# Token sums formed in place from PSUM, a fixed engine order behind the output product, each row normed with its residual

## The chip, the core and the metric

The kernel runs on one core of one Trainium2 chip. The metric is device time in microseconds (us), lower is better. A core has TensorE (PE, with its weight loads PEld), VectorE (DVE), ScalarE (ACT), GpSimd (POOL) and the queues that issue transfers (here mostly SP's). Each engine works through its own queue in order; they wait for each other on semaphores.

## What is computed

Two decoder layers on 1024 tokens of width 1024, float32. Each layer is a mixer, its output product, and a gated MLP, with an RMS norm before and after each half:

```python
for layer in range(2):
    y = mixer(rmsnorm(h, g[0]))                  # two mixers side by side, then one output product
    h = h + rmsnorm(y, g[1])
    y = conv_glu_ffn(rmsnorm(h, g[2]), w_up, conv_w, conv_b, w_down)
    h = h + rmsnorm(y, g[3])

def conv_glu_ffn(h, w_up, conv_w, conv_b, w_down):   # D_FF = 2816
    up = causal_depthwise_conv(h @ w_up, conv_w, conv_b)
    val, gate = split(up, 2)
    return (gelu(gate) * val) @ w_down
```

The change touches the stretch from the output product (`mix_out`) to the first chunk of the up product (`ffn`), and one place where the up product meets the down product (`down`). Both layers run the same code there.

## The kernel before

**Numbers in two parts.** Every operand of a large product is split into a high part (ACT, a copy to fp32r) and a low part (DVE, source minus high part): `split`, L88 to L90. `mm3` (L276) makes a product from three matmuls: high by high, high by low, low by high.

**The output product, `mix_out`.** Eight rows (t = 0 to 7) of 128 tokens. A row is 36 matmuls of 512 columns into a PSUM tile `pd`; then `residual` (row's sum of squares on ACT, a chain of small DVE operations for the root, two 1024-wide DVE operations, L270 and L271) and `prenorm` (again squares, root and L148). The norm of row t-1 is traced behind the residual of row t. `to_blocks` transposes a normed row on PE into a PSUM tile `pt` and splits it into the operands of the up product. Six rows go through `to_blocks` in `mix_out`, the last two in `ffn`.

**The up product, `ffn`.** It is a seven-product scheme on halves: tokens t < 4 and t >= 4, and input features in two halves. So it needs seven operands of tokens, `A[1]` to `A[7]`, and seven of weights for each of the 22 chunks of features. `A[1]` and `A[2]` are the plain first tokens, `A[4]` a negated part of the late tokens; `A[6]`, `A[7]`, `A[5]` and `A[3]` are differences and sums of an early and a late row (`sums`, `split_s4`). For them `to_blocks` keeps a copy `xr` of every row in SBUF (L386). The weights of a chunk arrive as two tiles `wr` (`up_raw`); `up_plain` splits the first (`w1`, for products 1 and 2), `up_sums` makes the others: `wt` for product 5, `w2` for 6 and 3, `w4` for 7 and 4. `prod` is one of the seven, 12 matmuls. Products 1 and 2 of a chunk (`p1`, `p2`) run LEAD = 2 chunks ahead of its other five (`chunk`).

So `ffn` starts with p1, p2 of chunks 0, 1 and 2, the last two rows' `to_blocks`, all token sums and chunk 0's weights; then it goes through `chunk(0)` to `chunk(21)`, each with products 6, 7, 5, 3 and 4 of its own and p1, p2 of the chunk two ahead (chunk 0 has none of these). A chunk ends with two convolutions, a gelu and the gating product L516, which is stored to DRAM.

**The down product, `down`,** is a generator. It prepares (loads, subtracts, splits: `prep`, L569) a list of operand pairs `made`, at first during the last two chunks.

**Order and room.** The program is traced in the order of the source; then a scheduler orders each engine's queue by its own estimate of times, and assigns buffers. `in_order` (L152), used at the kernel's start, ties PE's, ACT's and DVE's instructions of a block to the order in which they are traced. SBUF tiles come from two pools: `t4`, 21 tiles of 128x1024, and `t8`, 14 tiles of twice that (all 14 are the operands `A` from the first chunk on). PSUM has four tiles of 128x1024 (`ps`), for `pd`, `pt`, the accumulators `ac` of three chunks and `bb`.

Of the kernel before, what the change touches and what calls it, by code (L numbers as in the profile page):

```python
# [19 lines left out]
P = 128  # L20
# [25 lines left out]
class Trunk:  # L46
# [273 lines left out]
    def mix_out(self, layer, nk, hsrc, hdst):  # L320


        gpost = self.bcast(self.a["norm_g"][layer, 1], "gpost")
        gpre = self.bcast(self.a["norm_g"][layer, 2], "gpre", True)
        us = [self.unit(look=nk - 1 - j) for j in range(nk)]
        pend = []
        self.new_blocks(layer)
        for t in range(NT):
            sl = slice(t * P, (t + 1) * P)
            pd = self.PS("pd")  # L330
            for k in range(nk):
                for c in range(2):
                    cs = slice(c * 512, c * 512 + 512)
                    self.mm3(pd[:, cs], self.mix[k][0][:, sl], self.mix[k][1][:, sl], us[k][0][:, cs], us[k][1][:, cs], k == 0, k == nk - 1)
            hn = self.residual(t, pd, hsrc, hdst, gpost)
            if t:
                pend.append((t - 1, self.prenorm(last[0], gpre, last[1])))
            last = hn
            if t == 5:
                self.up_raw(0)  # L340
            if t == 6:
                self.up_plain(0)
            if t == 7:
                self.up_raw(1)
            if len(pend) > 1:
                self.to_blocks(*pend.pop(0))
        pend.append((NT - 1, self.prenorm(last[0], gpre, last[1])))
        return pend


# [16 lines left out]
    def to_blocks(self, t, xn):  # L367
        nc = self.nc
        pt = self.PS("pt").rearrange("p (k t) -> p k t", k=KD)
        for k in range(KD):  # L370
            nc.tensor.transpose(pt[:, k], xn[:, k * P:(k + 1) * P], self.ident)
        sl = slice(t % 4 * P, t % 4 * P + P)
        if t < 4:
            if t % 2 == 0:
                xr = self.T2("xr", F32, [P, 2, KD, P])
                self.xr[t], self.xr[t + 1] = xr[:, 0], xr[:, 1]
            for p in (1, 2):
                hi, lo = self.operand(p)
                self.split(hi[:, :, sl], lo[:, :, sl], pt[:, 4 * p - 4:4 * p])
        else:  # L380
            self.xr[t] = self.T("xr").rearrange("p (k t) -> p k t", k=KD)

            hi, lo = self.operand(4)
            nc.scalar.activation(hi[:, :, sl], pt[:, 4:], AF.Copy, scale=-1.0)
            nc.vector.scalar_tensor_tensor(lo[:, :, sl], pt[:, 4:], -1.0, hi[:, :, sl].bitcast(F32), op0=ALU.mult, op1=ALU.subtract)
        nc.scalar.activation(self.xr[t], pt, AF.Copy)  # L386

    def sums(self, t):


        v = self.nc.vector.tensor_tensor
        x, y = self.xr.pop(t - 4), self.xr.pop(t)
        sl = slice(t % 4 * P, t % 4 * P + P)
        if t % 2 == 0:
            self.s4 = self.T("s4").rearrange("p (j k t) -> p j k t", j=2, k=4)
        s32, s1 = (self.T("s").rearrange("p (j k t) -> p j k t", j=2, k=4) for _ in range(2))
        s3, s2, s1, s4 = s32[:, 0], s32[:, 1], s1[:, 0], self.s4[:, t % 2]
        v(s3, x[:, :4], y[:, :4], op=ALU.subtract)
        v(s2, y[:, 4:], s3, op=ALU.subtract)
        v(s1, y[:, :4], y[:, 4:], op=ALU.add)  # L400
        v(s4, x[:, 4:], s2, op=ALU.subtract)
        for p, src in ((6, s2), (7, s3), (5, s1)):
            hi, lo = self.operand(p)
            self.split(hi[:, :, sl], lo[:, :, sl], src)
        self.raw_sums[t] = s4

    def split_s4(self):
        hi, lo = self.operand(3)
        for t in range(4, NT):
            sl = slice(t % 4 * P, t % 4 * P + P)  # L410
            self.split(hi[:, :, sl], lo[:, :, sl], self.raw_sums[t])

    def up_raw(self, n):

# [12 lines left out]
        u[1], u[2] = self.parts(u["raw"][0], "w1")  # L427

    def up_sums(self, n):
        v = self.nc.vector.tensor_tensor  # L430
        u = self.up[n]
        r1, r2 = u.pop("raw")
        half = slice(0, 512)
        v(r2[:, half], r2[:, half], r1[:, half], op=ALU.subtract)
        t1 = self.T("wt", F32R)
        u[5] = t1[:, half], t1[:, 512:]
        self.split(*u[5], r2[:, half])
        v(r2[:, half], r2[:, 512:], r2[:, half], op=ALU.subtract)
# [13 lines left out]
    def ffn(self, layer, pend, hsrc, hdst, last):  # L452
        nc, a = self.nc, self.a
        add = lambda o, x, y: nc.vector.tensor_tensor(o, x, y, op=ALU.add)  # L454
        cw = self.small([P, 2 * NF, 4], "cw", bufs=1)
        nc.sync.dma_start(cw, a["ffn_cw"][layer])
        gd = [self.dr.tile([P, 2, 1024], F32, name=f"gd{layer}{m}") for m in range(NF // 2)]
        down = self.down(layer, gd, hsrc, hdst, last)
        lo, hi = slice(0, 512), slice(512, 1024)
        bb = {}  # L460

        def prod(out, n, p, first):
            w, x = self.up[n][p], self.A[p]
            for k in range(4):
                ks = slice(k * P, (k + 1) * P)
                self.mm3(out, w[0][:, ks], w[1][:, ks], x[0][:, k], x[1][:, k], first and k == 0, k == 3, True)

        def p1(n):
            u = self.up[n]
            u["ac"], u["val"], u["gate"] = self.PS("ac"), self.T("val"), self.T("gate")  # L470
            prod(u["ac"][:, lo], n, 1, True)
            nc.scalar.activation(u["val"][:, lo], u["ac"][:, lo], AF.Copy)

        def p2(n):
            u = self.up[n]
            if n % 2 == 0:
                bb[n // 2] = self.PS("bb")
            b = bb[n // 2][:, hi if n % 2 else lo]
            prod(b, n, 2, True)
            add(u["val"][:, lo], b, u["val"][:, lo])  # L480

        def chunk(n):
            u = self.up[n]
            val, gate = u["val"], u["gate"]
            A, C = u["ac"][:, lo], u["ac"][:, hi]
            m = n + LEAD
            if n == NF - 2:
# [5 lines left out]
            nc.scalar.activation(gate[:, hi], A, AF.Copy)
            add(gate[:, hi], C, gate[:, hi])
            if n and m < NF:
                p1(m)
            elif n:
                next(down)
            prod(A, n, 3, False)
            nc.scalar.activation(gate[:, lo], A, AF.Copy)  # L500
            if n and m < NF:
                p2(m)
            elif n:
                next(down)
            prod(C, n, 4, False)
            add(val[:, hi], C, val[:, hi])
# [21 lines left out]
        self.to_blocks(*pend.pop(0))
        self.sums(5)
        self.up_raw(2)  # L530
        self.sums(6)
        self.up_plain(2)
        p1(2)
        p2(2)
        self.sums(7)
        self.up_sums(0)
        self.split_s4()
        self.up_raw(3)
        for n in range(NF):
# [1077 lines left out]
```

## Time and profile before

| | us |
|---|---|
| median of 3 runs | 2282.49 (2278.32 to 2285.65) |
| the profiled execution | 2282.59 |
| its span | 2280.8 |
| PE busy in the span | 2161.2 |
| DVE busy in the span | 1589.6 |
| ACT busy in the span | 1050.7 |

The span is the time from the first instruction to the last in the trace, so 1.8 us of the profiled execution lie around it. A busy PE is not a PE at its peak: the array's clock has two levels, and the profile gives the granted clock of a stretch as a share of the full one.

### The profile page before, as it was taken

How to read it: one execution, taken by the hardware profiler on the slowest of the kernel's cores; microseconds unless marked ns; L12 is line 12 of the kernel's file. 1: busy time of each engine (PE TensorE's matmuls, PEld its weight loads, DVE VectorE, ACT ScalarE, POOL GpSimd, SP SyncE). 2: the span in 40 equal slices, each digit the busy share in tenths (PEclk: the TensorE clock that was granted, in tenths of full speed). 3: DMA queues.
4: the chain of work that ended last, by engine and by line, in shares of the span. 5: the costliest groups of instructions: out<-in, count | busy, mean ns of one | idle time of the engine just before them, and what ended most of it. 6: DMA issues, size and time to landing. Idle time of an engine off the chain costs nothing.

```text
span 2280.8 us, 25452 instructions
## 1 busy us (share of the span) xinstructions
PE 2161.2 (95%) x10096; PEld 1743.8 (76%) x10096; DVE 1589.6 (70%) x2083; ACT 1050.7 (46%) x1445; POOL 125.1 (5%) x101
## 2 busy tenths in 40 slices
PE   7899969999999999999999999999699999999997
PEld 6677847888887788788888877677588888877885
DVE  8877676777777787961234375667677777778787
ACT  5647444444445444540223375445454444444443
POOL 0550000000000000100000000410000000000001
PEclk9999979999999999999999999899799999999999
DMA  4012322222222530331011100434122222243304
GB/s 159 12 34 95 121 92 74 83 83 83 79 77 112 205 137 21 123 127 32 34 38 56 51 29 19 126 109 151 42 83 83 83 77 75 80 158 137 148 10 147
DMA packets 53896, 198.82 MB, mean 87 GB/s; under 512 B 7045, under 2 KB 8133, under 8 KB 51218
## 3 DMA queue, kind: packets, MB, share of 16 engines
q1 hardware_dynamic: 52130, 193.49, 23.7%
q0 software_dynamic: 1504, 3.46, 0.6%
q8 instruction: 79, 1.29, 0.2%
q14 instruction: 39, 0.32, 0.0%
q10 hardware_dynamic: 144, 0.26, 0.0%
HBM read 154.60 MB, written 41.99 MB: 86 GB/s over the span
## 4 chain that ended last, share of the span: by engine, by line
PE 47%; DVE 6%; ACT 3%; issue 1%; DMA 0%; DVEq 0%; SPq 0%; ACTq 0%
PE ac L279 5%; PE ac L281 5%; PE ac L280 5%; PE pj L279 4%; PE pj L280 4%; PE pj L281 4%; PE pd L280 3%; PE pd L279 3%; PE pd L281 3%; PE bb L279 1%; PE bb L280 1%; PE bb L281 1%; PE po L1242 1%; PE hpo L1454 1%; PE pi L279 1%
## 5 line engine op out<-in xcount | busy, mean ns | idle before, releaser
L279 PE MATMUL pj<-yh,wh 128*128 128x512 f32 (+1 forms) x672 | 266.6, 397 | 6.6 <-ACT s5uf L84 4.5
L280 PE MATMUL pj<-yl,wh 128*128 128x512 f32 (+1 forms) x672 | 260.9, 388 | 1.0 <-DVE yl L90 1.0
L281 PE MATMUL pj<-yh,wl 128*128 128x512 f32 (+1 forms) x672 | 259.5, 386 | 0.0
L280 PE MATMUL pd<-dwl,dgh 128*128 128x512 f32 x528 | 207.0, 392 | 6.8 <-DVE dwl L90 6.8
L281 PE MATMUL pd<-dwh,dgl 128*128 128x512 f32 x528 | 206.8, 392 | 0.0
L279 PE MATMUL pd<-dwh,dgh 128*128 128x512 f32 x528 | 206.3, 391 | 0.0
L279 PE MATMUL ac<-ah,w2h 128*128 128x512 f32 x352 | 143.9, 409 | 13.9 <-ACT w2h L89 11.1
L279 PEld LDWEIGHTS pj<-yh,wh 128*128 128x128 f32 x672 | 129.3, 192 | 34.1 <-ACT s5uf L84 4.7
L279 PE MATMUL ac<-ah,w4h 128*128 128x512 f32 x352 | 144.0, 409 | 5.5 <-ACT val L490 5.5
L280 PEld LDWEIGHTS pj<-yl,wh 128*128 128x128 f32 x672 | 129.0, 192 | 26.3 <-issue 3.4
L281 PEld LDWEIGHTS pj<-yh,wl 128*128 128x128 f32 x672 | 128.9, 192 | 25.6 <-issue 1.3
L281 PE MATMUL ac<-ah,w2l 128*128 128x512 f32 x352 | 139.6, 397 | 1.1 <-DVE w2l L90 1.1
L280 PE MATMUL ac<-al,w4h 128*128 128x512 f32 x352 | 139.1, 395 | 0.0
L280 PE MATMUL ac<-al,w2h 128*128 128x512 f32 x352 | 139.0, 395 | 0.0
L281 PE MATMUL ac<-ah,w4l 128*128 128x512 f32 x352 | 138.5, 393 | 0.0
L280 PEld LDWEIGHTS pd<-dwl,dgh 128*128 128x128 f32 x528 | 100.0, 189 | 28.5 <-DVE dwl L90 7.7
L281 PEld LDWEIGHTS pd<-dwh,dgl 128*128 128x128 f32 x528 | 100.0, 189 | 21.0
L279 PEld LDWEIGHTS pd<-dwh,dgh 128*128 128x128 f32 x528 | 99.5, 189 | 21.2 <-ACT dwh L89 0.4
L447 ACT ACTIVATE tv<-val,cw 128x1024 f32<-128x1024 f32 x44 | 54.8, 1246 | 127.9 <-DVE val L454 127.9
L89 ACT ACTIVATE dwh<-dw 128x1024 fp32r<-128x1024 f32 x66 | 69.9, 1059 | 93.0 <-PE pd L280 86.7
L515 ACT ACTIVATE tg<-tg 128x1024 f32<-128x1024 f32 x44 | 46.7, 1062 | 135.4 <-DVE tg L449 135.3
L649 POOL TENSOR_TENSOR acc<-acc,gpost 128x1024 f32<-128x1024 f32 x8 | 18.9, 2393 | 1512.9 <-ACT junk L646 1512.9
(441 smaller groups left out, 5151.9 us busy)
## 6 DMA issues: line engine op xcount, KB each, us to landing
wr<-in_WU_dram SPq DMA_DIRECT2D x88, 512.0 KB, 4.2
raw<-in_W_dram SPq DMA_DIRECT2D x56, 512.0 KB, 3.7
gd<-tv SPq DMA_DIRECT2D x44, 512.0 KB, 2.6
dg<-gd SPq DMA_DIRECT2D x20, 1024.0 KB, 5.1
dw<-in_WD_dram SPq DMA_DIRECT2D x20, 1024.0 KB, 7.6
h<-h SPq DMA_DIRECT2D x28, 512.0 KB, 4.3
h<-hn SPq DMA_DIRECT2D x20, 512.0 KB, 2.9
h<-in_x_dram SPq DMA_DIRECT2D x16, 512.0 KB, 4.7
```

Source lines behind the costliest of these rows:

```text
L89: self.nc.scalar.activation(hi, src, AF.Copy)
L279: mm(out, lhsT=lh, rhs=rh, start=first, stop=False, skip_group_check=chain)
L280: mm(out, lhsT=lh, rhs=rl, start=False, stop=False, skip_group_check=chain)
L281: mm(out, lhsT=ll, rhs=rh, start=False, stop=last, skip_group_check=chain)
L447: nc.scalar.activation(t0, src, AF.Identity, scale=cw[:, c, 2:3], bias=cw[:, c, 3:4])
L515: nc.scalar.activation(tg, tg, AF.Gelu_apprx_tanh)
L649: nc.gpsimd.tensor_tensor(acc[t], acc[t], gpost, op=ALU.mult)
L1242: nc.tensor.matmul(po[cols, c, at], lhsT=V(ku)[:, c, cols], rhs=st[:, hp, j], start=j == 0, stop=j == 1)
L1454: nc.tensor.matmul(po[rs, t], lhsT=qi[:, n * 64:n * 64 + 64], rhs=st[(n - 1) // 8][:, (n - 1) % 8], start=False, stop=True)
```

## The change

1. `mix_out`: row t is normed right behind its own residual instead of behind the residual of row t+1. The rows still wait two deep for `to_blocks`.
2. `to_blocks` for t >= 4 makes no copy of the row. It takes three sums on DVE straight from the PSUM tile: two into one new SBUF tile, the third in place over the early row's copy. `split_sum` splits one kind of sum for a list of rows; the sum for `A[3]` is made there, in place.
3. `up_sums` is cut in two: up to `w2` (`up_sums1`), and `w4` (`up_sums2`).
4. The start of `ffn` is traced in another order, under `in_order`; chunk 2's weights are requested first.
5. `chunk(0)` runs its last products as 5, 4, 3 and copies product 7 out first.
6. In `down`, the pairs number 4 to 11 are prepared under `issue_after` the last gating product: their DVE instructions stand behind it in DVE's queue.

```diff
             hn = self.residual(t, pd, hsrc, hdst, gpost)
-            if t:
-                pend.append((t - 1, self.prenorm(last[0], gpre, last[1])))
-            last = hn
+            pend.append((t, self.prenorm(hn[0], gpre, hn[1])))
...
-            if len(pend) > 1:
+            if len(pend) > 2:
                 self.to_blocks(*pend.pop(0))
-        pend.append((NT - 1, self.prenorm(last[0], gpre, last[1])))
...
-        else:
-            self.xr[t] = self.T("xr").rearrange("p (k t) -> p k t", k=KD)
...
-        nc.scalar.activation(self.xr[t], pt, AF.Copy)
...
+            nc.scalar.activation(self.xr[t], pt, AF.Copy)
+            return
+        hi, lo = self.operand(4)
+        nc.scalar.activation(hi[:, :, sl], pt[:, 4:], AF.Copy, scale=-1.0)
+        nc.vector.scalar_tensor_tensor(lo[:, :, sl], pt[:, 4:], -1.0, hi[:, :, sl].bitcast(F32), op0=ALU.mult, op1=ALU.subtract)
+        v = nc.vector.tensor_tensor
+        x = self.xr[t - 4]
+        y = self.xr[t] = self.T("xs").rearrange("p (k t) -> p k t", k=KD)
+        v(y[:, :4], x[:, :4], pt[:, :4], op=ALU.subtract)
+        v(y[:, 4:], pt[:, 4:], y[:, :4], op=ALU.subtract)
+        v(x[:, :4], x[:, :4], y[:, 4:], op=ALU.add)
+    def split_sum(self, p, rows):
+        src = {6: lambda x, y: y[:, 4:], 7: lambda x, y: y[:, :4], 5: lambda x, y: x[:, :4], 3: lambda x, y: y[:, 4:]}[p]
+        if p == 3:
+            for t in rows:
+                y = self.xr[t][:, 4:]
+                self.nc.vector.tensor_tensor(y, self.xr[t - 4][:, 4:], y, op=ALU.subtract)
+        hi, lo = self.operand(p)
+        for t in rows:
             sl = slice(t % 4 * P, t % 4 * P + P)
-            self.split(hi[:, :, sl], lo[:, :, sl], self.raw_sums[t])
+            self.split(hi[:, :, sl], lo[:, :, sl], src(self.xr[t - 4], self.xr[t]))
...
             prod(C, n, 7, True)
+            if n == 0:
+                nc.scalar.activation(gate[:, hi], C, AF.Copy)
             prod(A, n, 5, False)
...
+            if n == 0:
+                add(gate[:, hi], A, gate[:, hi])
+                prod(C, n, 4, False)
+                add(val[:, hi], C, val[:, hi])
+                prod(A, n, 3, False)
+                nc.scalar.activation(gate[:, lo], A, AF.Copy)
...
-        p1(0)
-        p2(0)
-        self.to_blocks(*pend.pop(0))
-        self.up_plain(1)
-        self.sums(4)
-        p1(1)
-        p2(1)
-        self.to_blocks(*pend.pop(0))
-        self.sums(5)
         self.up_raw(2)
-        self.sums(6)
-        self.up_plain(2)
-        p1(2)
-        p2(2)
-        self.sums(7)
-        self.up_sums(0)
-        self.split_s4()
+        with self.in_order():
+            p1(0)
+            p2(0)
+            self.up_plain(1)
+            self.up_sums1(0)
+            self.to_blocks(*pend.pop(0))
+            self.split_sum(6, (4, 5, 6))
+            p1(1)
+            p2(1)
+            self.up_plain(2)
+            self.to_blocks(*pend.pop(0))
+            self.split_sum(6, (7,))
+            p1(2)
+            self.up_sums2(0)
+            p2(2)
+            self.split_sum(7, range(4, NT))
+            self.split_sum(5, range(4, NT))
+            self.split_sum(3, range(4, NT))
         self.up_raw(3)
...
-            made.append(prep(b, p, len(made) > len(steps) // 2))
+            wide = len(made) > len(steps) // 2
+            if 4 <= len(made) < 12:
+                with self.tc.issue_after(self.gated.ins if hasattr(self.gated, "ins") else self.gated):
+                    made.append(prep(b, p, wide))
+            else:
+                made.append(prep(b, p, wide))
```

## Rows read from the trace of the kernel before

**Rows 1.** The page, first part: busy us, share of the span, instructions.

```profile
PE 2161.2 (95%) x10096; PEld 1743.8 (76%) x10096; DVE 1589.6 (70%) x2083; ACT 1050.7 (46%) x1445; POOL 125.1 (5%) x101
```

**Rows 2.** Four stages of layer 0: stretch, length, busy (count) by engine, granted clock.

```profile
core 0: us, PE busy (x) PEld busy (x) DVE busy (x) ACT busy (x) POOL busy (x), PEclk, DMA share, GB/s
217.65:288.60 70.95, 70.95 (x338) 59.09 (x337) 45.67 (x102) 33.94 (x61) 0.00 (x0) 1.00 0.33 113
288.60:332.95 44.35, 24.43 (x91) 18.55 (x90) 34.02 (x62) 22.70 (x39) 0.00 (x0) 0.74 0.31 105
332.95:356.31 23.36, 20.70 (x67) 15.20 (x68) 11.49 (x13) 6.22 (x8) 0.00 (x0) 0.76 0.14 46
356.31:450.00 93.69, 93.68 (x408) 75.58 (x407) 71.46 (x74) 47.46 (x56) 0.00 (x0) 1.00 0.20 74
```

**Rows 3.** What PE waited for, whole span: total us, times, longest.

```profile
PE ac L279 <- ACT w1h L89: 24.9, 4, 9.0
...
PE pd L280 <- DVE dwl L90: 6.8, 2, 3.4
```

**Rows 4.** PE in order of time, layer 0: start, us, instruction, idle before.

```profile
288.61 0.48 PE L279 MATMUL ac<-ah,w1h 128*128 128x512 f32 x1
...
296.24 1.66 PE L371 MATMUL pt<-cst,h 128*128 128x128 f32 x8 [1.94 <-DVE h L148]
...
319.54 0.80 PE L279 MATMUL ac<-ah,w1h 128*128 128x512 f32 x1 [9.04 <-ACT w1h L89]
...
332.95 0.79 PE L279 MATMUL ac<-ah,w2h 128*128 128x512 f32 x1 [5.53 <-ACT w2h L89]
...
356.50 0.39 PE L281 MATMUL ac<-ah,w2l 128*128 128x512 f32 x1
```

**Rows 5.** Two stretches behind a wait, columns as in Rows 2.

```profile
301.30:306.80 5.50, 5.48 (x14) 4.33 (x15) 4.39 (x6) 0.63 (x1) 0.00 (x0) 0.50 0.89 278
...
332.90:344.00 11.10, 9.80 (x21) 6.82 (x22) 4.72 (x6) 1.66 (x2) 0.00 (x0) 0.50 0.00 0
```

**Rows 6.** ACT in order of time, layer 0.

```profile
300.22 1.05 ACT L89 ACTIVATE w1h<-wr 128x1024 fp32r<-128x1024 f32 x1
...
318.45 1.04 ACT L89 ACTIVATE w1h<-wr 128x1024 fp32r<-128x1024 f32 x1
```

**Rows 7.** DVE groups, 288.6 to 356.6: count, busy us, mean ns, idle before.

```profile
L398 DVE TENSOR_TENSOR s<-xr 128x512 f32<-128x512 f32 x4 | 2.7, 686 | 0.0
...
L148 DVE SCALAR_TENSOR_TENSOR h<-hn,rn,gpre 128x1024 f32<-128x1024 f32 x2 | 2.6, 1278 | 0.0
...
L385 DVE SCALAR_TENSOR_TENSOR al<-pt,ah 128x512 fp32r<-128x512 f32 x3 | 2.1, 686 | 1.0 <-ACT ah L384 1.0
```

**Rows 8.** DVE in order of time: two neighbours of each width.

```profile
302.44 0.68 DVE L398 TENSOR_TENSOR s<-xr 128x512 f32<-128x512 f32 x1
303.05 0.68 DVE L400 TENSOR_TENSOR s<-xr 128x512 f32<-128x512 f32 x1
...
333.46 1.22 DVE L90 TENSOR_TENSOR w2l<-wr,w2h 128x1024 fp32r<-128x1024 f32 x1
334.59 0.69 DVE L90 TENSOR_TENSOR al<-s,ah 128x512 fp32r<-128x512 f32 x1
```

**Rows 9.** SP's queue in order of time, layer 0.

```profile
286.74 1.26 SPq L417 DMA_DIRECT2D wr<-in_WU_dram  x2
...
300.48 0.33 SPq L124 DMA_DIRECT2D gpre<-in_norm_g_dram  x1
300.91 26.68 SPq L417 DMA_DIRECT2D wr<-in_WU_dram  x4
```

**Rows 10.** PE in layer 1: its first up-product matmul, and chunk 1's.

```profile
1584.86 0.48 PE L279 MATMUL ac<-ah,w1h 128*128 128x512 f32 x1
...
1650.47 0.39 PE L281 MATMUL ac<-ah,w2l 128*128 128x512 f32 x1
```

**Rows 11.** DVE where the up product meets the down product, layer 0.

```profile
763.33 1.23 DVE L573 TENSOR_TENSOR dw<-dw 128x1024 f32<-128x1024 f32 x1 [3.03 <-DMA dw<-in_WD_dram]
764.47 0.69 DVE L454 TENSOR_TENSOR val<-ac,val 128x512 f32<-128x512 f32 x1
```

More of the change, by code (lines that the diff above doesn't have):

```diff
@@ L379, in to_blocks @@
                 self.split(hi[:, :, sl], lo[:, :, sl], pt[:, 4 * p - 4:4 * p])
-        else:
-            self.xr[t] = self.T("xr").rearrange("p (k t) -> p k t", k=KD)
-            hi, lo = self.operand(4)
-            nc.scalar.activation(hi[:, :, sl], pt[:, 4:], AF.Copy, scale=-1.0)
-            nc.vector.scalar_tensor_tensor(lo[:, :, sl], pt[:, 4:], -1.0, hi[:, :, sl].bitcast(F32), op0=ALU.mult, op1=ALU.subtract)
-        nc.scalar.activation(self.xr[t], pt, AF.Copy)
[L388 to L405, printed above, removed]
@@ L407, in split_s4 @@
-    def split_s4(self):
-        hi, lo = self.operand(3)
-        for t in range(4, NT):
+            nc.scalar.activation(self.xr[t], pt, AF.Copy)
[6 more added lines that the diff above has]
+        y = self.xr[t] = self.T("xs").rearrange("p (k t) -> p k t", k=KD)
@@ L429, in up_sums, with up_sums1 @@
     def up_sums(self, n):
+        self.up_sums1(n)
+        self.up_sums2(n)
+    def up_sums1(self, n):
         v = self.nc.vector.tensor_tensor
         u = self.up[n]
-        r1, r2 = u.pop("raw")
+        r1, r2 = u["raw"]
         half = slice(0, 512)
@@ L438, in up_sums, with up_sums2 @@
         v(r2[:, half], r2[:, 512:], r2[:, half], op=ALU.subtract)
+        u[6], u[3] = self.parts(r2, "w2")
+    def up_sums2(self, n):
+        u = self.up[n]
+        r1, r2 = u.pop("raw")
         r1 = r1.rearrange("p (j c) -> p j c", j=2)
-        v(r1, r2[:, half].unsqueeze(1).to_broadcast([P, 2, 512]), r1, op=ALU.subtract)
-        u[6], u[3] = self.parts(r2, "w2")
+        self.nc.vector.tensor_tensor(r1, r2[:, :512].unsqueeze(1).to_broadcast([P, 2, 512]), r1, op=ALU.subtract)
         u[7], u[4] = self.parts(r1.rearrange("p j c -> p (j c)"), "w4")
@@ L491, in chunk @@
             prod(C, n, 7, True)
+            if n == 0:
+                nc.scalar.activation(gate[:, hi], C, AF.Copy)
             prod(A, n, 5, False)
[L493 to L506, printed above, removed]
+            if n == 0:
[5 more added lines that the diff above has]
+            else:
+                nc.scalar.activation(gate[:, hi], A, AF.Copy)
+                add(gate[:, hi], C, gate[:, hi])
+                p1(m) if m < NF else next(down)
+                prod(A, n, 3, False)
+                nc.scalar.activation(gate[:, lo], A, AF.Copy)
+                p2(m) if m < NF else next(down)
+                prod(C, n, 4, False)
+                add(val[:, hi], C, val[:, hi])
             if m + 1 < NF:
@@ L515, in chunk @@
             nc.scalar.activation(tg, tg, AF.Gelu_apprx_tanh)
-            nc.vector.tensor_tensor(tv, tv, tg, op=ALU.mult)
+            self.gated = nc.vector.tensor_tensor(tv, tv, tg, op=ALU.mult)
             nc.sync.dma_start(gd[n // 2][:, n % 2], tv)
             self.up.pop(n)
-        p1(0)
-        p2(0)
-        self.to_blocks(*pend.pop(0))
-        self.up_plain(1)
-        self.sums(4)
-        p1(1)
-        p2(1)
-        self.to_blocks(*pend.pop(0))
-        self.sums(5)
-        self.up_raw(2)
-        self.sums(6)
-        self.up_plain(2)
-        p1(2)
-        p2(2)
-        self.sums(7)
-        self.up_sums(0)
-        self.split_s4()
+        self.up_raw(2)
+        with self.in_order():
[16 more added lines that the diff above has]
+            self.split_sum(3, range(4, NT))
         self.up_raw(3)
@@ L618, in more @@
                 load(b, {2: 1, 1: 0}[p])
-            made.append(prep(b, p, len(made) > len(steps) // 2))
+            wide = len(made) > len(steps) // 2
+            if 4 <= len(made) < 12:
+                with self.tc.issue_after(self.gated.ins if hasattr(self.gated, "ins") else self.gated):
+                    made.append(prep(b, p, wide))
+            else:
+                made.append(prep(b, p, wide))
         def room(cap):
```

## The prediction

> **What bounds the kernel now.** The busy shares come first: PE holds 95% of the span and DVE 70% [rows 1], so the time is PE's, except where PE waits or runs at its lower clock. The next view is the stages. In the output product PE is busy without a gap at the full clock (70.95 of 70.95 us). From the first up-product matmul (288.6) to chunk 1 (356.5) it is not: 24.43 busy of 44.35 us, then 20.70 of 23.36, at a granted clock of 0.74 and 0.76. From chunk 1 on it is full again, 93.68 of 93.69 [rows 2]. So the change can find time only in that stretch of 67.9 us, which comes back in layer 1 as 1584.9 to 1650.5, 65.6 us [rows 10].
>
> What would PE need there? A matmul costs 93.69/408 = 0.23 us in the dense stage [rows 2]. The stretch holds six products of 12 in p1 and p2, chunk 0's five products, and two transposed rows of some 0.8 us (an estimate, half of the row's 1.66 at half the clock [rows 4]): 16.6 + 13.8 + 1.6 = 32.0 us. Thus 35.9 us are lost in layer 0 and 33.6 in layer 1.
>
> The view of PE in order of time says where. The two longest waits are 9.04 us for the high part `w1h` and 5.53 for `w2h` [rows 4]; `w1h` costs 24.9 us in four waits, two per layer [rows 3]. [...]
>
> Why is `w1h` late? ACT's rows show chunk 1's at 300.22 and chunk 2's at 318.45 [rows 6], behind the splits of sums that no product needs yet: the queue's order, not ACT's load (22.70 busy of 44.35 [rows 2]). DVE is the fuller of the two with 34.02 of 44.35. So the order is to blame first, and DVE's own work is what remains when the order is right.
>
> **The change, part by part.**
>
> *Prices.* On DVE, operations issue 0.60 us apart at 512 columns (302.44 to 303.05) and 1.14 at 1024 (333.46 to 334.59) [rows 8]; a 1024-wide operation with two scalars takes 1.28 [rows 7], say 1.2 from issue to issue (an estimate, its overlap taken as the others').
>
> *The copies and the sums.* Eight 1024-wide ACT copies go. ACT has idle time throughout [rows 2], so I take zero. DVE keeps four operations for each late row; two of them now read PSUM. L385 reads PSUM and takes 686 ns, L398 reads SBUF alone and takes 686 [rows 7]: no price. [...]
>
> *The norm next to its residual.* No instruction is added. A row's chain (squares, root, L270, L271, squares, root, L148) lies beside a row of 36 matmuls, and PE transposes a row only two rows later; DVE has 25.3 us idle in that stage and ACT 37 [rows 2]. So zero in `mix_out`; the three sums of rows 4 and 5 ride in the same idle time, those of row 5 partly behind 288.6. Without that cover PE would wait for `pt`, at most the 4 x 0.60 us of one row.
>
> *The transfer of chunk 2's weights.* Before, it stands in SP's queue behind `gpre` (issued 300.48) at 300.91; chunk 1's were issued at 286.74 [rows 9]. Traced first, it can go next to chunk 1's as soon as the output product frees its tiles. It is needed at about 305, so even the old place would cost only 0 to 3 us; I take 0.
>
> *The new order.* This is the sum. I follow DVE from 288.6, since every gate of PE now stands in its queue:
> a) the end of row 7 (two roots of some 1.0 us as an estimate, L270, L271 and two L148, one of row 6) and row 5's four: 2.0 + 4.7 + 2.4 = 9.1;
> b) add, `w1l(1)`, `up_sums1` (3 x 0.60 + 1.14), row 6's four, three splits, add, `w1l(2)`: 0.6 + 1.1 + 2.9 + 2.4 + 1.8 + 0.6 + 1.1 = 10.5, and one wait of 1.1 for ACT's `w2h`. At 288.6 + 20.7 = 309.3 PE has what p1(2) needs;
> c) row 7's four, a split, `w4` (two of 1.14): 5.3 and 1.1 for ACT's `w4h`, until 315.7. Then DVE's next add waits for p2(2). PE's p1(2) and p2(2) take 24 x 0.23 = 5.5 at the full clock, until 314.8, or 24 x 0.47 = 11.3 at half, until 320.6;
> d) the add, then splits for 7 and 5, subtractions and splits for 3: 0.6 + 16 x 0.60 = 10.2. PE does products 6, 7 (waits for its split), 5, 4 and 3 beside it;
> e) chunk 0's two adds, `w1l(3)`, and chunk 1's weights to `w2l`: 1.2 + 1.1 + 1.8 + 2.3 = 6.4.
> Chunk 1 starts at 315.7 + 16.6 = 332.3, or 320.6 + 16.6 = 337.2 with the low clock in c. PE will have been idle some 2 us at a time before p1(2) (it waits for `w1l(1)`, for `pt` and for `w1l(2)`), and 1.94 us idle were enough before for eight transposes to take 1.66 us [rows 4]; so I take the middle, 334.7. That is 21.8 us less than 356.5. The same 46.1 us from layer 1's start give 1631.0 against 1650.5, 19.5 less [rows 10]. What is late next is `w2l` of chunk 1, by about 4 us.
>
> *Chunk 0's order.* Product 4 no longer waits for the gate's add; a wait of about a microsecond goes, inside the stretch, and step d covers it. Not counted again.
>
> *The last gating product.* In `down` DVE's subtraction waited 3.03 us for a transfer and the chunk's add stood behind it (763.33, 764.47) [rows 11]. Moved behind L516, this frees the add by some 0.4 us and puts two operations of 1.14 later. PE's one wait here, 3.4 us for `dwl` in each layer [rows 3], is for pair 3, which is not moved. The bounds are 3.4 gained and 2.3 lost per layer; the rows are nearest to none, so zero.
>
> **Sum.** 2282.6 (the profiled execution; its span is 2280.8, the 1.8 us around it stay) - 21.8 - 19.5 = 2241.3 us. That execution lies within 0.1 us of the median of the runs, so nothing is corrected: 2241. With chunk 1 at 331 to 340 the same sum gives 2234 to 2252.
>
> **The rivals.**
>
> 1. *PE stays at half clock.* The order cuts PE's work into bursts between waits of 2 us. If the 108 matmuls behind p2(0) (which ends at 288.6 + 24 x 0.23 = 294.1) all ran at 0.47 us with some 3 us of waits, chunk 1 would start at 294.1 + 50.8 + 3 = 348: 8.5 less in layer 0, 6.2 in layer 1, 2268. For it speaks the 11.1 us at 0.50 [rows 5]; against it, that the second half of the stretch is now nearly one dense run. [...]
>
> 2. *A transfer for chunk 1's stage comes late.* `t4` has 21 tiles; before `w4` of chunk 0 I count 21 in use (six `wr`, `wt`, two `w2`, two `w1`, six `val` and `gate`, four sums), so chunk 3's weights may have to wait until the sums are split, at the end of d. Two tiles of 512 KB at the 278 GB/s of a stretch here [rows 5] are an estimated 3.8 us, ACT's `w1h` another 1.05 [rows 6], and `w1l(3)` stands ahead of chunk 1's weights on DVE: 3.7 us more per layer beside the adds, 2249. Against it: `wr` of chunk 0 is free right after `w4`.
>
> 3. *DVE loses less.* If DVE never waits for ACT (2.2) and `w1l(3)` gives way (1.1), chunk 1 starts at 332.3 - 3.3 = 329: 27.5 and 25.2 less, 2230. It needs the full clock throughout.
>
> 4. *It does nothing.* The scheduler still places row 7 and chunk 0 around the fixed block; if PE waits for these as long as for the old order, 2282.
>
> 5. *Slower: PE and DVE take turns.* Adds that wait for p2 now stand in DVE's queue ahead of the weights that PE waits for. If nothing overlapped, the stretch would take PE's 32.0 and DVE's 9.1 + 10.5 + 5.3 + 10.2 + 6.4 = 41.5, together 73.5 us against 67.9 and 65.6: 5.6 and 7.9 slower, 2296. It decides where less than 6 us (8 in layer 1) of the 32 overlap. Against it: in each round `w1l` comes right after the add, and PE works while DVE does the rest of the round.
>
> **How the numbers follow.** The forecast (2234 to 2252) has 0.55, rival 1 0.13, rival 2 0.08, rival 3 0.10, rival 4 0.07, rival 5 0.07. The range 2224 to 2268 takes in the forecast and rivals 1 to 3, and leaves out 4 and 5 and the tails. About 0.3% (6.8 us) is what three runs can tell from no change. Faster: 0.55 + 0.13 + 0.08 + 0.10 = 0.86; same 0.07; slower 0.07.
>
> **What would show it.** In the changed kernel: chunk 1's first matmul some 46 us behind the first matmul of p1(0), in both layers; `w1h(2)` on ACT at about 304 in place of 318.45; no wait of PE over 4 us in the stretch; DVE idle there below 8 us; the last wait before chunk 1 for DVE's `w2l`. The output product should stay free of gaps, and the 3.4 us for `dwl` should stay. The prediction is wrong if DVE's queue shows waits for PE or for tiles that I didn't count, if the clock stays at 0.50 beyond p2(2), or if the time won is given back in the chunks behind.

## The result and the profile after

The changed kernel takes 2246.7 us (median of 4 runs, 2245.4 to 2248.7) against 2282.25 for the kernel before in the same session (2278.3 to 2285.7): a ratio of 0.9846, 95% interval 0.9827 to 0.9864. The forecast was 2241, range 2224 to 2268. The profiled execution took 2247.86 us, its span 2246.1.

The page's first part, against [rows 1]: PE is busy for as long as before (2161.2), so the gain is time in which PE stood still.

```profile
PE 2159.4 (96%) x10096; PEld 1745.3 (78%) x10096; DVE 1590.2 (71%) x2083; ACT 1044.3 (46%) x1437; POOL 124.6 (6%) x101
```

The stages of layer 0 (columns as in [rows 2]): the output product, two pieces of the stretch that the change rewrites, the chunks behind it. The last two rows run from the first up-product matmul to the start of DVE's `w2l` of chunk 1, in each layer.

```profile
219.70:290.70 71.00, 71.00 (x338) 59.10 (x337) 49.33 (x104) 35.66 (x62) 0.00 (x0) 1.00 0.33 113
290.70:320.60 29.90, 24.18 (x94) 18.29 (x93) 26.39 (x48) 14.16 (x27) 0.00 (x0) 0.83 0.42 148
320.60:336.20 15.60, 13.24 (x55) 9.65 (x54) 15.53 (x25) 8.95 (x16) 0.00 (x0) 1.00 0.06 17
336.20:450.00 113.80, 113.57 (x495) 91.70 (x494) 86.20 (x89) 56.77 (x68) 0.00 (x0) 1.00 0.23 83
...
290.70:336.30 45.60, 37.52 (x147) 28.04 (x146) 42.02 (x72) 23.22 (x42) 0.00 (x0) 0.89 0.30 103
...
1565.60:1611.70 46.10, 37.01 (x146) 27.91 (x145) 42.01 (x71) 22.98 (x41) 0.00 (x0) 0.89 0.27 90
```

The output product is as dense as before, although DVE does 3.7 us more work in it. In the rewritten stretch DVE is now the full engine: 42.02 of 45.60 us, 3.6 idle. The same piece of the kernel before, from p1(0) to `w2l` of chunk 1, lasted 64.5 us, and DVE was idle for 21.5 of it:

```profile
288.60:353.10 64.50, 41.92 (x144) 31.24 (x142) 43.02 (x72) 27.47 (x46) 0.00 (x0) 0.74 0.22 73
```

DVE's work hardly shrank (43.0 to 42.0); its idle time did. What PE waited for, over the whole span, against [rows 3]: `w1h` fell from 24.9 to 5.1 us, `dwl` stayed.

```profile
PE pd L280 <- DVE dwl L90: 6.8, 2, 3.4
...
PE ac L279 <- ACT w1h L89: 5.1, 2, 2.6
...
PE ac L279 <- DVE val L453: 4.1, 2, 2.1
```

PE in order of time, layer 0, the rows that answer [rows 4]: p1(0), the longer waits of the stretch, and of chunk 1's first product the first matmul, the third (the second of the pair at 339.30) and the last. ACT's copy of chunk 0's product 3 stands below them.

```profile
290.72 0.48 PE L279 MATMUL ac<-ah,w1h 128*128 128x512 f32 x1
...
299.87 0.79 PE L279 MATMUL ac<-ah,w1h 128*128 128x512 f32 x1 [2.57 <-ACT w1h L89]
...
309.62 1.06 PE L368 MATMUL pt<-cst,h 128*128 128x128 f32 x8 [0.78 <-DVE xs L388]
...
312.75 0.61 PE L279 MATMUL ac<-ah,w1h 128*128 128x512 f32 x1 [2.07 <-DVE val L453]
...
324.04 0.50 PE L279 MATMUL ac<-ah,w4h 128*128 128x512 f32 x1 [1.07 <-ACT val L489]
...
327.80 0.50 PE L279 MATMUL ac<-ah,wt 128*128 128x512 f32 x1 [0.75 <-ACT gate L492]
...
332.10 0.50 PE L279 MATMUL ac<-ah,w4h 128*128 128x512 f32 x1 [0.53 <-DVE gate L453]
...
335.87 0.40 PE L279 MATMUL ac<-ah,w2h 128*128 128x512 f32 x1
...
339.30 0.62 PE L281 MATMUL ac<-ah,w2l 128*128 128x512 f32 x2
...
341.56 0.39 PE L281 MATMUL ac<-ah,w2l 128*128 128x512 f32 x1
```

```profile
339.72 0.60 ACT L500 ACTIVATE gate<-ac 128x512 f32<-128x512 f32 x1 [0.94 <-PE ac L281]
```

Waits of 9.04 and 5.53 us have become waits of at most 2.6. To compare chunk 1's start, the same matmul has to be taken in both kernels. PE runs the first two matmuls of chunk 1's first product, which need `w2h` alone, ahead of the end of chunk 0, and the rest behind it. In the kernel before, the first is at 353.18, and the 356.50 of [rows 4] (in layer 1 the 1650.47 of [rows 10]) is the third, the first that needs `w2l`:

```profile
353.18 0.47 PE L279 MATMUL ac<-ah,w2h 128*128 128x512 f32 x1
```

In the changed kernel the first is at 335.87. Then PE finishes chunk 0's product 3 (ACT copies it at 339.72), and the third is the second of the pair at 339.30, so at 339.53: 48.8 us behind p1(0), against 67.9 before. In layer 1 it is 49.4, against 65.6.

**The yardstick below.** Several parts are worth 1 to 4 us a layer, and whole runs scatter by as much. So each kernel is also measured within its trace: from the first matmul of p1(0) to ACT's copy of chunk 3's first product. This row is at 397.08 before and 379.95 after:

```profile
397.08 0.58 ACT L490 ACTIVATE val<-ac 128x512 f32<-128x512 f32 x1
```
```profile
379.95 0.58 ACT L489 ACTIVATE val<-ac 128x512 f32<-128x512 f32 x1
```

That is 108.5 and 89.2 us behind p1(0), 19.2 won; in layer 1 106.2 and 89.8, 16.4 won. To the end of the up product the gains are 20.3 and 16.3 (475.5 to 455.2, and 472.6 to 456.3). The span is 34.7 shorter; 1.8 went outside this stretch (the output product of layer 0 already starts 2.1 us later).

The kernels of the table were measured in four sessions, each beside the kernel before, which took 2277.8 to 2282.8 us in them; so whole times are compared by their ratio and not by their medians. The times within the trace come from one execution of each kernel. Its two layers run the same code and differ by up to 2.3 us there, so a difference of less than 1 us is not settled by them. "DVE" below is the time from p1(0) to the start of chunk 1's `w2l` in layer 0 and the idle part of it.

| kernel | median us | ratio to before (95%) | chunk 3 at, layers 0 / 1 | DVE: length, idle |
|---|---|---|---|---|
| before | 2277.8 to 2282.8 | 1 | 108.5 / 106.2 | 64.5, 21.5 |
| sums in place alone | 2263.6 | 0.9927 (0.9909 to 0.9946) | 98.2 / 98.7 | 54.2, 12.6 |
| the same, ACT copies kept | 2265.1 | 0.9932 (0.9912 to 0.9952) | 99.1 / 98.7 | 55.2, 12.2 |
| sums and fixed order | 2252.0 | 0.9873 (0.9856 to 0.9891) | 91.3 / 90.1 | 47.0, 4.2 |
| **after: the whole change** | 2246.7 | 0.9846 (0.9827 to 0.9864) | 89.2 / 89.8 | 45.6, 3.6 |
| ACT copies kept | 2247.1 | 0.9848 (0.9828 to 0.9868) | 89.8 / 89.9 | 46.2, 4.2 |
| old place of the norm | 2249.4 | 0.9877 (0.9861 to 0.9893) | 90.1 / 90.1 | 46.5, 3.3 |
| old order of chunk 0 | 2245.8 | 0.9864 (0.9847 to 0.9882) | 90.5 / 90.0 | 45.0, 3.6 |
| no fixed order | 2241.6 | 0.9825 (0.9806 to 0.9843) | 85.4 / 85.1 | 40.7, 2.1 |
| row 4's splits early | 2247.5 | 0.9857 (0.9840 to 0.9875) | 88.4 / 88.4 | 42.9, 2.9 |
| and weights ahead of splits | 2249.0 | 0.9866 (0.9845 to 0.9886) | 88.5 / 88.4 | 42.9, 2.9 |
| and no fixed order | 2240.5 | 0.9839 (0.9824 to 0.9855) | 85.5 / 85.2 | 40.7, 2.1 |
| eight more DVE operations | 2261.8 | 0.9914 (0.9893 to 0.9936) | 95.9 / 95.9 | 52.1, 5.2 |
| eight of them on GpSimd | 2251.5 | 0.9878 (0.9857 to 0.9899) | 93.7 / 91.8 | 46.6, 6.2 |

### The profile page after: what moved, and what is told of

Read it like the earlier page. It is cut to its first block, busy times and chain, and to the rows that moved or that the text cites. A ratio compares the mean times of both kernels' runs of the same rounds, so it can differ in the third digit from the quotient of the medians.

```text
span 2246.1 us, 25455 instructions
## 1 busy us (share of the span) xinstructions
PE 2159.4 (96%) x10096; PEld 1745.3 (78%) x10096; DVE 1590.2 (71%) x2083; ACT 1044.3 (46%) x1437; POOL 124.6 (6%) x101
## 4 chain that ended last, share of the span: by engine, by line
PE 49%; DVE 5%; ACT 2%; issue 1%; DVEq 0%; ACTq 0%
PE ac L279 5%; PE ac L281 5%; PE ac L280 5%; PE pj L279 4%; PE pj L280 4%; PE pj L281 4%; PE pd L280 4%; PE pd L279 4%; PE pd L281 4%; PE bb L281 1%; PE bb L279 1%; PE bb L280 1%; PE po L1253 1%; PE pi L280 1%; PE pi L279 1%
## 5 line engine op out<-in xcount | busy, mean ns | idle before, releaser
L279 PEld LDWEIGHTS pj<-yh,wh 128*128 128x128 f32 x672 | 131.5, 196 | 33.9 <-ACT s5uf L84 4.1
L660 POOL TENSOR_TENSOR acc<-acc,gpost 128x1024 f32<-128x1024 f32 x8 | 18.9, 2392 | 1472.9 <-ACT junk L657 1472.9
```

Source lines behind the costliest of these rows:

```text
L279: mm(out, lhsT=lh, rhs=rh, start=first, stop=False, skip_group_check=chain)
L660: nc.gpsimd.tensor_tensor(acc[t], acc[t], gpost, op=ALU.mult)
```

## The experiments

### Which part gained

**The sums in place alone**, on the kernel before: three sums in `to_blocks` (two of them read PSUM, the third SBUF alone), splits where `sums(4)` to `sums(7)` stood. Of the other parts only the cut of `up_sums` in two comes with it; DVE keeps the old order there (subtraction for `w4`, then `w2l`: 332.32 and 333.46 before, 322.21 and 323.35 here).

```diff
-            nc.scalar.activation(self.xr[t], pt, AF.Copy)
...
+            v(y[:, :4], x[:, :4], pt[:, :4], op=ALU.subtract)
+            v(y[:, 4:], pt[:, 4:], y[:, :4], op=ALU.subtract)
+            v(x[:, :4], x[:, :4], y[:, 4:], op=ALU.add)
```

> Only the sums made from PSUM in place; order at the start of the up stage, norm, chunk 0 and the down stage as before. Mine (the copies cost ACT only time that it had): 2276 to 2284 us, the stage at 474 to 477 us in layer 0. Rival (the copies on ACT made w1h late): a fourth or more of the gain, 2272 us or less, with w1h(2) some 5 us sooner than 29.9 us after p1(0).

2263.6 us, and 10.2 and 7.5 us at chunk 3: half of the whole gain. My theory, that the gain is the fixed order's and the sums bring nothing, falls here. DVE's rows of this kernel, the first sums of rows 4, 5 and 6, and ACT's `w1h` of chunk 2 and `w2h` of chunk 0:

```profile
287.55 0.68 DVE L390 TENSOR_TENSOR xs<-xr,pt 128x512 f32<-128x512 f32 x1
...
295.47 0.68 DVE L390 TENSOR_TENSOR xs<-xr,pt 128x512 f32<-128x512 f32 x1
...
298.71 0.68 DVE L390 TENSOR_TENSOR xs<-xr,pt 128x512 f32<-128x512 f32 x1
```
```profile
311.84 1.04 ACT L89 ACTIVATE w1h<-wr 128x1024 fp32r<-128x1024 f32 x1
...
321.73 1.06 ACT L89 ACTIVATE w2h<-wr 128x1024 fp32r<-128x1024 f32 x1 [0.49 <-DVE wr L436]
```

Row 4's sums began at 302.44 before [rows 8]; here they begin at 287.55, where DVE was idle for 2.16 us before. `w1h(2)` comes at 311.84 instead of 318.45 [rows 6]. But the edit has two sides: sums made earlier, and copies gone from ACT. So the next kernel keeps the copies.

**The copies kept**, once with the sums alone and once in the changed kernel, with the same edit:

```diff
+        nc.scalar.activation(y, pt, AF.Copy)
-        v(y[:, :4], x[:, :4], pt[:, :4], op=ALU.subtract)
-        v(y[:, 4:], pt[:, 4:], y[:, :4], op=ALU.subtract)
+        v(y[:, :4], x[:, :4], y[:, :4], op=ALU.subtract)
+        v(y[:, 4:], y[:, 4:], y[:, :4], op=ALU.subtract)
```

> The kernel with only the sums in place (2263.6 us), but with each late row copied by ACT from PSUM to SBUF again, and the sums made at once from that copy. It splits that gain in two. Theory A (the gain comes from making the sums when the row comes, so that rows 4 and 5's six operations and their waits leave DVE's queue behind p1(0)): 2261 to 2268 us, the stage from p1(0) to the end of the up product at 464 to 468 us. Theory B (it comes from ACT's queue, from which the copies of 1.02 us left): 2274 us or more, the stage at 472 us or more, w1h(2) some 29 us after p1(0) again.

> The changed kernel, but each late row is copied from PSUM to SBUF by ACT again and DVE's two operations read the copy. Mine (no price of its own for PSUM reads, ACT has room): 2244 to 2251 us, DVE's operations keep their 0.60 us spacing. [...] Rival (ACT's copy stands ahead of the next w1h): w1h(2) 1 to 3 us later and the stage longer by as much, 2250 to 2256.

By ratio 0.9932 against 0.9927, and 0.9848 against 0.9846; at chunk 3 at most 0.9 us. Whether DVE reads PSUM or a copy, and whether ACT copies, is worth nothing here that can be measured; making the sums when the row comes is worth 9.4 and 7.5 us with the copies kept. (With it the sums take fewer SBUF tiles, and the one for `A[3]` is made later; these were not separated from the time at which the sums are made.) The copies move waits all the same: with the sums alone PE waits 10.7 us for `w1h` in the whole span, with the copies kept 19.3, and the rest of the stretch takes that up. In the changed kernel with copies `w1h` is no later, and PE's transposes wait for the copy (2.58 us) instead of for DVE's sums (0.78).

**Sums and fixed order**, without the three small parts: the changed kernel with the norm a row behind, chunk 0's products in the old order, and `if 4 <= len(made) < 12` never true.

> The sums in place from PSUM and the fixed order, with the old place of the norm, the old order of chunk 0 and no gate on the last gating products' preparation. Mine (order is all): 2244 to 2253 us, the stage from p1(0) to the end of the up product within 2 us of 455.2 in layer 0; where it is longer, row 7's norm or chunk 0's gate add shows as a PE wait of 1 to 3 us before chunk 1. Rival (the norm beside its residual is what lets the rows' transposes come in time): 3 to 8 us longer per layer, 2254 to 2265.

2252.0 us: the new order adds 7.0 and 8.6 us at chunk 3, and the three small parts together 2.0 and 0.3. `dwl` costs 6.8 us here as well, so the gating of `down`'s preparation leaves that wait as it was; from the end of layer 0's up product to layer 1's p1(0) the changed kernel takes 819.6 us and this one 819.1. The gating was not run by itself. The stage from p1(0) to the end of the up product, 457.9 and 458.1 us, is 2.7 and 1.8 longer than the changed kernel's: the time is mine, but in layer 0 the stage is longer than the 2 us that I allowed.

**The norm's and chunk 0's old places**, each alone in the changed kernel:

```diff
-            pend.append((t, self.prenorm(hn[0], gpre, hn[1])))
+            if t:
+                pend.append((t - 1, self.prenorm(last[0], gpre, last[1])))
+            last = hn
...
```
```diff
-            if n == 0:
-                nc.scalar.activation(gate[:, hi], C, AF.Copy)
...
-                add(gate[:, hi], A, gate[:, hi])
-                prod(C, n, 4, False)
-                add(val[:, hi], C, val[:, hi])
-                prod(A, n, 3, False)
...
+            prod(A, n, 3, False)
+            nc.scalar.activation(gate[:, lo], A, AF.Copy)
...
+            prod(C, n, 4, False)
+            add(val[:, hi], C, val[:, hi])
```

> The changed kernel with the old place of the norm alone (a row's norm one row behind its residual). Mine (the norm's place is worth nothing): the end of chunk 3's first product at 89 to 90 us behind p1(0), 2244 to 2250 us. Rival (the three parts put back together cost 5 us, and it is the norm, since row 6's late norm holds back PE's transposes): 91 us or more, 2249 to 2254 us.

> The changed kernel with the old order of chunk 0's products and gate alone. Mine (covered by DVE's work for product 3): within 0.5 us of 89.3 us to the end of chunk 3's first product, 2244 to 2250 us. Rival (a PE wait of one to two us for the gate's add comes back before product 4): 90.5 us or more, 2248 to 2253 us.

The norm is worth 0.9 and 0.3 us, chunk 0's order 1.3 and 0.2. Neither shows in the whole time. The norm went a little over what I allowed (90.1 against 90). With chunk 0 I expected 0.5 us at most: layer 0 has the rival's time (90.5), layer 1 mine (90.0), and PE's rows have no wait for the gate's add before product 4 in layer 0, so the rival's reason isn't shown.

### What the fixed order itself does

The changed kernel with the scheduler free, then two attempts to find what the freedom gains, then the second of them free:

```diff
         self.up_raw(2)
-        with self.in_order():
+        if True:
             p1(0)
```

> The changed kernel with the same lines in the same trace order, but without the fixed order at the start of the up stage (the scheduler places them). Mine (the fixed order is what brings chunk 2's weights ahead of the later sums): most of the gain goes, ACT makes w1h(2) after the splits again, p1(0) to the end of the up product is within 5 us of before's 475.5 in layer 0, 2270 to 2282 us. Rival (the trace order alone is enough, because the scheduler follows it): 455 us for that stage, 2245 to 2250. Rival (the gain is from the sums made from PSUM): also 2245 to 2255, since these stay.

2241.6 us, and 3.8 and 4.7 us less at chunk 3 (3.3 and 3.5 to the end of the up product): the scheduler follows the new trace order closely enough, and tying the queues to it costs. My theory fell; the first rival was right that the trace order is enough, and the kernel is quicker than it said. DVE's rows of this kernel: row 4's splits run before p1(0) (291.8) and just behind it, row 5's splits fill gaps, and `w1l(2)` starts 19.1 us behind p1(0), against 21.8 in the changed kernel.

```profile
289.36 0.68 DVE L90 TENSOR_TENSOR al<-xs,ah 128x512 fp32r<-128x512 f32 x1
...
291.09 0.69 DVE L90 TENSOR_TENSOR al<-xs,ah 128x512 fp32r<-128x512 f32 x1
...
303.75 0.69 DVE L90 TENSOR_TENSOR al<-xs,ah 128x512 fp32r<-128x512 f32 x1
...
310.87 1.22 DVE L90 TENSOR_TENSOR w1l<-wr,w1h 128x1024 fp32r<-128x1024 f32 x1
```

With row 4's splits traced ahead of the fixed block:

```diff
         self.up_raw(2)
+        for p in (6, 7, 5, 3):
+            self.split_sum(p, (4,))
         with self.in_order():
...
-            self.split_sum(7, range(4, NT))
...
+            self.split_sum(7, range(5, NT))
...
```

> The changed kernel with the fixed order, but row 4's four splits and its subtraction for product 3 traced ahead of the fixed block, where the scheduler may place them beside the output product. Theory A (leaving the order free gained 5 us because such work could be done in DVE's idle time there, 5 x 0.60 = 3.0 us per layer): the stage 452 to 453.5 us, 2240 to 2243 us, about as without the fixed order. Rival (the free order gains because PE keeps its clock, or w1h(1) isn't behind row 7's squares): within 1 us per layer of the changed kernel, 2245 to 2249.

and with the splits of rows 5 and 6 behind chunk 2's weights as well:

```diff
-            self.split_sum(6, (5, 6))
             p1(1)
             p2(1)
             self.up_plain(2)
+            self.split_sum(6, (5, 6))
```

> The fixed order kept, row 4's splits ahead of it (as in the run before), and the splits of rows 5 and 6 for product 6 put behind chunk 2's weights instead of ahead of them. In the kernel without a fixed order, chunk 3 begins 4 us sooner behind p1(0) than in the changed kernel (85.4 against 89.3 us in layer 0, by the end of the chunk's first product); row 4's splits gave 0.8 to 1.4 of it. Theory A (the rest is w1l(2), which stands behind three splits in the fixed order and came at 21.8 us there, at 19.1 without it): w1l(2) at about 20 us, p1(2) sooner by 1.2 to 1.8 us, that end at 86 to 87 us in both layers, 2240 to 2244 us. Rival (the free order gains by something else, and product 6's splits are now late): 88 us or more, 2245 to 2250 us.

Each theory fell in turn. Row 4's early splits shorten DVE's way to `w2l` by 2.7 us (45.6 to 42.9) but chunk 3 comes only 0.8 and 1.4 sooner; weights ahead of splits bring p1(2) 1.2 us sooner and chunk 3 not at all. Why shows in the second kernel: ACT's copy of `gate` stands in its queue behind product 3's four splits, those wait for DVE's subtractions, and PE waits for the copy. ACT's rows, then PE's:

```profile
323.34 2.19 ACT L89 ACTIVATE ah<-xs 128x512 fp32r<-128x512 f32 x4 [2.56 <-DVE xs L398]
325.43 0.57 ACT L492 ACTIVATE gate<-ac 128x512 f32<-128x512 f32 x1
```
```profile
326.06 0.50 PE L279 MATMUL ac<-ah,wt 128*128 128x512 f32 x1 [2.22 <-ACT gate L492]
```

This wait is 0.75 us in the changed kernel, so 1.5 of what was won in front is lost here, and PE still has chunk 0's products 5, 4 and 3 to do behind it. Without the fixed order the subtractions come 30.6 us behind p1(0) (33.9 here), because row 5's splits were done in gaps where the fixed queue waits for `w2h` and `w4h` (1.13 and 1.19 us). That the filled gaps are the rest of the difference is read from these rows and was not isolated.

> The lines of the run before in the same trace order, without the fixed order. Theory A (with weights first and ready splits early in the trace, the scheduler has nothing more to gain or lose): as the kernel without a fixed order, the end of chunk 3's first product at 84.5 to 86 us, 2238 to 2243 us. Rival (it moves work back ahead of the weights): 87 to 90 us, 2244 to 2248 us.

2240.5 us and 85.5 / 85.2 at chunk 3: as without the fixed order alone, and these two are the quickest. Both have DVE idle for only 2.1 us. Their ratios overlap with that of the whole change, so on whole runs they are not clearly apart; within the traces the 3.8 to 4.7 us a layer stand well clear.

### Is DVE's queue the bound?

Eight operations more, and eight fewer, in each layer's stretch:

```diff
             self.split(hi[:, :, sl], lo[:, :, sl], src(self.xr[t - 4], self.xr[t]))
+            if p in (7, 5):
+                self.nc.vector.tensor_tensor(lo[:, :, sl], src(self.xr[t - 4], self.xr[t]), hi[:, :, sl].bitcast(F32), op=ALU.subtract)
```

> The changed kernel with the low parts of products 7 and 5 made twice: eight more operations of 0.60 us on DVE in each layer's stretch before chunk 1, at a place where PE has other work. If DVE's queue is the bound of the stretch, as forecast, chunk 1 starts 4.8 us later in both layers: the stage 459 to 461 us, 2254 to 2258 us. Rival (PE with its clock and ACT's weights bound it): 0 to 1.5 us per layer, 2246 to 2250 us.

Chunk 3 comes 6.7 and 6.1 us later for 4.8 us of work (and the kernel takes 2261.8 us, more than I allowed): work added to DVE's queue is paid in full, so it is the bound for more work. The surplus is DVE's idle time, up from 3.6 to 5.2. For less work it is not the only one: the 2.7 us taken off its way to `w2l` above gave 0.8 and 1.4.

The same count goes to GpSimd; `split` takes the engine of its subtraction as a last argument here:

```diff
...
-                self.nc.vector.tensor_tensor(y, self.xr[t - 4][:, 4:], y, op=ALU.subtract)
+                self.nc.gpsimd.tensor_tensor(y, self.xr[t - 4][:, 4:], y, op=ALU.subtract)
...
-            self.split(hi[:, :, sl], lo[:, :, sl], src(self.xr[t - 4], self.xr[t]))
+            self.split(hi[:, :, sl], lo[:, :, sl], src(self.xr[t - 4], self.xr[t]), self.nc.gpsimd if p == 3 else None)
```

> The changed kernel with product 3's four subtractions and four low parts on GpSimd: 4.8 us less for DVE in each layer's stretch. If DVE's queue is the bound: chunk 1 sooner by 2 to 4.8 us per layer (2.4 us of PE's idle time lie behind p2(2)), 2238 to 2243 us. Rival (those of PE's waits that are left stand ahead of product 3): 0 to 1 us per layer, 2245 to 2249. Rival (GpSimd is late with product 3's operands, or slows DVE while it runs): PE waits for GpSimd before chunk 1, 2247 to 2260.

Slower, 4.4 and 2.0 us at chunk 3: the last rival. GpSimd's rows of this kernel, then DVE's beside them:

```profile
310.37 5.48 POOL L398 TENSOR_TENSOR xs<-xr,xs 128x512 f32<-128x512 f32 x3 [128.87 <-DVE al L90]
...
327.78 6.74 POOL L90 TENSOR_TENSOR al<-xs,ah 128x512 fp32r<-128x512 f32 x4 [7.47 <-ACT ah L89]
```
```profile
309.55 2.95 DVE L90 TENSOR_TENSOR al<-xs,ah 128x512 fp32r<-128x512 f32 x3
...
331.61 1.77 DVE L90 TENSOR_TENSOR wt<-wr,wt 128x512 fp32r<-128x512 f32 x1
```

The same two groups in the changed kernel:

```profile
310.12 1.89 DVE L90 TENSOR_TENSOR al<-xs,ah 128x512 fp32r<-128x512 f32 x3
...
333.08 0.69 DVE L90 TENSOR_TENSOR wt<-wr,wt 128x512 fp32r<-128x512 f32 x1
```

DVE's operations beside GpSimd's take 1.77 us for 0.69, and 2.95 for three instead of 1.89. While GpSimd makes product 3's four low parts (until 334.5), DVE waits 2.02 us for ACT's `w1h`, and its `w1l`, `wt` and the subtraction L433 take 4.87 us instead of 2.60. The gate's add stands behind all this here and starts 44.9 us behind p1(0) instead of 40.6, and PE waits for it, 1.82 us instead of 0.53:

```profile
335.73 0.50 PE L279 MATMUL ac<-ah,w4h 128*128 128x512 f32 x1 [1.82 <-DVE gate L453]
```

## Why the prediction was right, and where it was off

**What bounds it.** "The queue's order, not ACT's load": shown. ACT's copies can stay (0 to 0.9 us), DVE's work is nearly the same (43.0 and 42.0 us), and its idle time fell from 21.5 to 3.6 us. That DVE's own work remains when the order is right: shown by the eight added operations, though behind the gate's add PE's own products (332.10 to 339.53) end later than DVE's `w2l` (337.50).

**The sum.** DVE's queue came out nearly as forecast: `w2l` of chunk 1 was to be done 46.1 us behind p1(0) and was done at 46.8 in layer 0 and 47.4 in layer 1. The term that was mis-sized is the step from there to PE, "that is 21.8 us less than 356.5". It takes the end of DVE's `w2l` as the moment at which PE begins, and sets it against a time of PE's before. PE took `w2l` up 2.0 us after its end in both layers, because it was still at work on chunk 0's product 3 and on p2(3); in the kernel before it was 2.1 us, for `w2l` ended at 354.37 there and PE's matmul is at 356.50:

```profile
353.14 1.23 DVE L90 TENSOR_TENSOR w2l<-wr,w2h 128x1024 fp32r<-128x1024 f32 x1
```

So 21.8 and 19.5 were forecast at chunk 1, and 19.1 and 16.2 measured: 6.0 of the 6.6 us between 2241.3 and the profiled execution's 2247.86. To the end of the up product 1.2 came back, and the 1.8 above went elsewhere.

**Inside it, errors cancelled.** Step b was to end with `w1l(2)` at 20.7 us and ended at 23.0. The scheduler had put three subtractions L429 there, two of them for chunks 1 and 2 (2 x 0.60 us), and row 7's root. DVE in order of time, layer 0:

```profile
299.46 0.68 DVE L429 TENSOR_TENSOR wr<-wr,wr 128x512 f32<-128x512 f32 x1
...
300.14 1.21 DVE L90 TENSOR_TENSOR w1l<-wr,w1h 128x1024 fp32r<-128x1024 f32 x1
...
301.33 0.69 DVE L429 TENSOR_TENSOR wr<-wr,wr 128x512 f32<-128x512 f32 x1
...
302.00 0.69 DVE L429 TENSOR_TENSOR wr<-wr,wr 128x512 f32<-128x512 f32 x1
...
306.33 1.23 DVE L90 TENSOR_TENSOR w2l<-wr,w2h 128x1024 fp32r<-128x1024 f32 x1 [1.13 <-ACT w2h L89]
...
312.52 1.22 DVE L90 TENSOR_TENSOR w1l<-wr,w1h 128x1024 fp32r<-128x1024 f32 x1
...
319.38 1.23 DVE L90 TENSOR_TENSOR w4l<-wr,w4h 128x1024 fp32r<-128x1024 f32 x1 [1.19 <-ACT w4h L89]
320.52 0.69 DVE L453 TENSOR_TENSOR val<-bb,val 128x512 f32<-128x512 f32 x1
...
331.35 0.69 DVE L453 TENSOR_TENSOR gate<-ac,gate 128x512 f32<-128x512 f32 x1
...
336.28 1.22 DVE L90 TENSOR_TENSOR w2l<-wr,w2h 128x1024 fp32r<-128x1024 f32 x1
```

Step c ended at 29.8 instead of 27.1; but the add behind it then found p2(2) done, so the 2.4 us set aside for PE's lower clock were not needed. (Step c's 0.47 us a matmul at half the clock is 9.80/21 of [rows 5]; p1(2) and p2(2) took 7.35 us here, at a granted 0.77 on average, between its 5.5 and 11.3.) Steps d and e took 10.8 and 6.2 against 10.2 and 6.4. That DVE's total came out within 1.3 us is in part luck: a lateness of 2.7 us in front stood against a reserve of 2.4 that was meant for something else. Of the signs, `w1h(2)` came 19.8 us behind p1(0), not 15.4, and PE's last wait before chunk 1 is not for `w2l` but for the gate's add (0.53 us at 332.10); DVE's idle time, the longest wait, the output product and `dwl` came as said.

**The steps taken at zero.** The copies and PSUM reads: right. DVE's sums from PSUM take 0.68 us, those from SBUF the same, and the kernels with copies are not quicker (ratios 0.9848 against 0.9846, and 0.9932 against 0.9927). The sums among them: wrong as a part by itself. They were worth 10.2 and 7.5 us without the new order; the forecast's walk along DVE's queue had them early and so put their gain on the order. The total was right, its split was not. The norm (0.9 and 0.3), chunk 0's order (1.3 and 0.2) and the gating (the wait for `dwl` is as it was): small, as said. Chunk 2's weights were requested with chunk 1's, and nothing waited for them: right.

**The rivals.** In layer 0 PE's granted clock was 0.50 behind its wait of 2.57 us, for 5.9 us, and 0.53 behind the one of 2.07, for 3.3; it was 0.83 in the first 29.9 us on average and 1.00 from 320.6 on. So rival 1 took place for a small part. Rival 2: no wait for a transfer. Rivals 4 and 5 did not happen. Rival 3's time, 2230, was not reached even without a fixed order (2240).

**What the list missed:** that fixing the order costs. DVE waits 1.13 and 1.19 us for ACT there by design, and ready splits stand behind it; I counted these waits and did not ask what a free queue would do with them.

## What to carry to other kernels

In a stretch where several engines feed PE by turns, follow the fullest engine's queue from the first gate to the last and count its idle time: here 21.5 us of idle time were the gain to be had (17.9 of the 18.9 us by which DVE's way to `w2l` became shorter are idle time), and work moved to GpSimd or taken off ACT was not. Compare like with like: the end of one engine's work is not the moment at which another takes it up, and here 2 us lay between them in both kernels. Make a sum when its row comes rather than when it is needed; and once the trace order is right, test whether the queues need to be tied to it, for here the scheduler left DVE 2.1 us idle where the fixed order left 3.6. A later engine's queue decides as well: here 1.5 us of what DVE gained in front was lost, because ACT's copy stood behind work that still waited for DVE.

## What the runs showed of the chip

DVE beside GpSimd. In the kernel with eight operations on GpSimd, a 128x512 operation with both inputs in SBUF took 1.77 us on DVE beside them; the same one took 0.69 in the changed kernel. Two operations with one input in PSUM kept their time (0.68 us for the add at 312.42, 0.67 for the sum at 315.23, while GpSimd worked from 310.37 to 315.85). What makes the difference isn't shown. Nor is it shown whether DVE slows GpSimd: its own 128x512 operations took 1.83 us (5.48 for three), 2.15 (one) and 1.69 (6.74 for four) here, and groups of such operations in the mixer of the kernel before take it from 1.25 to 2.15 on average.

The same wait was followed by different clocks. Behind PE's wait of 2.57 us for `w1h`, at the same place of the same code, the granted clock of the next 6 us was 0.50 in the changed kernel and 1.00 in the one with GpSimd, 12 matmuls against 22:

```profile
299.87:305.80 5.93, 5.62 (x12) 3.97 (x13) 5.33 (x11) 1.33 (x3) 0.00 (x0) 0.50 0.03 11
```
```profile
299.29:305.30 6.01, 5.21 (x22) 4.01 (x23) 5.34 (x11) 1.41 (x3) 0.00 (x0) 1.00 0.05 10
```

In layer 1 of the changed kernel it was 0.71, over 5.89 us. What this is worth at the end of the stretch was not isolated. An average between 0.50 and 1.00 mixed the two in the kernel before: from 288.6 to 353.6 the granted clock of 130 pieces of 0.5 us was 0.50 in 65, 1.00 in 59 and something between in 6.
